# Hybrid decoder trunk on one core: maxima of weight strips over the partitions by a TensorE product and VectorE instead of GpSimd, and an earlier place for the maximum of a feed-forward strip

## The chip, the cores and the metric

The kernel runs on one core of one Trainium2 chip. The metric is the device time of one execution, in microseconds. A core has TensorE (PE, matrix products; its weight loads are shown apart as PEld), VectorE (DVE), ScalarE (ACT), GpSimdE (POOL) and the queues that issue transfers (SP's and POOL's among them). Each engine works through its own list of instructions in order and waits on semaphores of the others.

## The reference

Two layers of a decoder trunk in float32 over 1024 prompt tokens with 16 meta tokens ahead of them, and 8 running sequences of one token each. Each layer is a mixer and a feed-forward net, each with a norm before and after it:

```python
def sq_relu_mlp(x, w1, w2):
    h = jax.nn.relu(x @ w1)
    return (h * h) @ w2

h = rms_norm(x, p["norm_mix_pre"][i])
m = ssd_mixer(h, ...) if i % 2 == 0 else rglru_mixer(h, ...)   # layer 0 / layer 1
x = x + rms_norm(m, p["norm_mix_post"][i])
h = rms_norm(x, p["norm_ffn_pre"][i])
x = x + rms_norm(sq_relu_mlp(h, w1[i], w2[i]), p["norm_ffn_post"][i])
```

The width is 1024, the feed-forward width 4096. Prompt and sample tokens go through the kernel together, 1048 columns in three chunks of 350, 350 and 348.

## The kernel before

**Stages.** The core runs four stages one after the other: the SSD mixer, feed-forward net 0, the LRU mixer, feed-forward net 1. In the profile the SSD mixer takes about the first 930 us, feed-forward net 0 lies between 930 and 1700, the LRU mixer between 1700 and 2080, and the rest is feed-forward net 1.

**Products in float16 parts.** Every float32 operand is split in a float16 part hi and the rest lo, after a scaling by a power of two that makes it fit. A product takes three passes: hi by hi, hi by lo, lo by hi.

**Strips.** The weights come in strips of 256 columns, `[128, 8 x 256]` float32, 1 MB each, into the ring `ws` of two buffers. For each strip its largest magnitude is found (`rm`, the maxima on each partition; `wgb`, the maximum over the partitions on all of them). From it come the scale `sw` and its inverse `winv` by way of `qw` and `pw` (one column each, on DVE), and the strip is converted to the tile `wh` (hi by ACT, lo by DVE). The list `specs` gives the order of the strips and their kind: `a` takes a bound from the sums that ACT accumulates, `d` and `h` take the largest magnitude by one DVE reduce of 128 x 2048, `s` one that a kind `g` found long before.

**The feed-forward net.** It runs in four blocks of 1024 hidden units. A block has four strips of the first weight (kind `h` in block 0, `H` in the others) and then four of the second (kind `S` in blocks 0 to 2, `2` in block 3). Kinds `H` and `S` are multiplied by Winograd's form, seven products for eight. For these, three quarters of the strip are converted as they are into the tile `wp` (hi by ACT, lo by DVE), then POOL forms four sums in the room of the strip (`ws<-ws`), and the sums are converted into `wh`. All four pairs of K tiles of an `H` strip are summed, two of the four pairs of an `S` strip. Kinds `S` and `2` also carry the factors `rj` of the hidden rows, so their maximum is a reduce in two halves (`r4`), a product with `rj` and a small reduce (`rm`). One unit of an `H` or `S` strip is one chunk of tokens; a strip has three units. In a unit DVE adds the products up from PSUM into `z` (rows `z<-z,mm`), and then come the square of the hidden units (`H`, and `HT`, their sums) or the addition to the output `acc`. In block 0 POOL also forms the sums of the input (`f`), and where hidden units are summed, POOL's rows `z<-z` do it.

**Who sets the order.** The strips' pipeline is the generator `wlane`: it is advanced by one step (`tick`) beside each bundle of products, and `wneed` runs it on until the strip is there. It loads strip i+1 and then converts strip i. Within what dependences allow, a scheduler orders each engine's list anew, so the order on an engine isn't that of the program text. Almost every instruction is issued through one helper, so nearly all of them carry line L89 in the profile, and the names of the tiles tell them apart.

**The maximum over the partitions.** In `strip_scale` it is a library function of POOL, `partition_all_reduce`, of one column. There are 109 strips with such a maximum: 33 before feed-forward net 0, 32 in each feed-forward net, and 12 in the LRU mixer.

Of the kernel before, what the change touches and what calls it, by code (L numbers as in the profile page):

```python
# [11 lines left out]
F16 = mybir.dt.float16  # L12
I32 = mybir.dt.int32
AF = mybir.ActivationFunctionType
OP = mybir.AluOpType
AX = mybir.AxisListType
# [20 lines left out]
NSUM = 2  # L37
RBUF = 4
# [15 lines left out]
def cols(c):  # L54
    """The columns of a chunk of tokens."""
    return slice(c * CW, c * CW + WC[c])


class Carve:
    """Small float32 tiles cut from larger ones."""  # L60
# [17 lines left out]
class Queue:  # L78
    """An engine; while hold is set its instructions are issued in program order, and later ones behind them."""
# [38 lines left out]
class Body:  # L118
# [7 lines left out]
    # ------------------------------------------------------- order of work  # L126
    def tick(self):
        """One step of every piece of work that runs beside the matrix products."""
        for lane in list(self.lanes):
            if next(lane, self) is self:  # L130
                self.lanes.remove(lane)
# [5 lines left out]
    def tab(self, *args, **kw):  # L137
        """An activation whose function needs a table set: these stay in program order."""
# [13 lines left out]
    # ---------------------------------------------------------------- setup  # L152
    def setup(self):
# [28 lines left out]
        # pre-norm gains and group-norm gains scaled by a power of two so that hi/lo fit float16  # L182
# [13 lines left out]
        # the inputs of the ffn leave room for sums of four  # L196
# [48 lines left out]
    def pow2(self, b, n, pool, tag):  # L245
        """p = the power of two at or below b; s = 2^14 / p."""
# [9 lines left out]
    # -------------------------------------------------------------- weights  # L256
# [5 lines left out]
    def strip_scale(self, gmax):  # L262
        nc, ty = self.nc, self.tiny
        gb = ty.tile([P, 1], F32, tag="wgb", name="wgb")
        nc.gpsimd.partition_all_reduce(gb, gmax, P, RED.absmax)
        s, p = self.pow2(gb, 1, ty, "w")
        inv = ty.tile([P, 1], F32, tag="winv", name="winv", bufs=8)
        nc.vector.tensor_scalar(inv, p, 2.0 ** -14, None, op0=OP.mult)
        return s, inv, gb

    def split(self, w, st, s, parts):
        """w = float16 hi and lo parts of st * s, s [P, parts] by contiguous column ranges."""
# [12 lines left out]
    def wconv(self, st, kind, cols=SW):  # L285
        """A strip of weights as float16 hi and lo parts [P, 2, KT, cols], the factor that undoes its scaling and,
        for kinds h and H, the factor of its hidden units. Kind a takes a bound from the sums of the magnitudes, kind s
        one that kind g found before; kinds 2 and S carry the factors of the hidden rows. Kinds H and S are for the
        products by Winograd's form: with the quarters that are used as they are."""
        nc, ty = self.nc, self.tiny  # L290
        w = self.wh.tile([P, 2, KT * cols], F16, tag="wh", name="wh") if kind != "g" else None
        if kind in "HS":
            npair = 4 if kind == "H" else NSUM
            wp = self.wh.tile([P, 2, KT * cols], F16, tag="wh", name="wp")[:, :, :3 * npair * P]
            wp = wp.rearrange("p s (q k c) -> p s q k c", q=3, c=P)
        rm = ty.tile([P, 1], F32, tag="rm", name="rm")
        parts = 1
        if kind == "a":
            nc.scalar.activation(w[:, 0], st, AF.Abs, accum_out=rm)
# [25 lines left out]
        yield  # L325
        if kind in "HS":
            s, inv = self.quarter(s, inv)
# [12 lines left out]
    def quarter(self, s, inv):  # L340
        """Scales that leave room for sums of four."""
# [7 lines left out]
    def sums(self, wp, st, s, npair, parts):  # L349
        """Steps: the quarters of a strip [K tiles, M] that are used as they are, A11, A12, A22 (A ij: m tile i, k  # L350
        tiles of parity j), as float16 parts in wp; then the sums of Winograd's form in the room of the strip. Only
        the first npair pairs of k tiles."""
# [20 lines left out]
    def product(self, ps, i, w, B, T, npair):  # L373
        """ps = one of the seven products of quarters over the first pairs of k tiles, three passes of the float16
        parts; open for the products of the other pairs where there are any."""
# [14 lines left out]
    def quadrant(self, w, B, npair, i, l):  # L390
        """The operands of m tile i by half l of the tokens over the other pairs."""
# [7 lines left out]
    def wlane(self):  # L399
        def load(src, kind, cols=SW):  # L400
# [3 lines left out]
        for i in range(len(self.specs)):  # L404
            cost = {"H": 2, "S": 2, "g": 0}.get(self.specs[i][1], 1)
# [4 lines left out]
            yield from self.wconv(*staged.pop(i))  # L410
# [7 lines left out]
    def hidden_scale(self, wmax, inv):  # L418
        """The factors of one strip's hidden units: t = 2^7, or 2^6 where the squares are summed, / (power of two at or
        below the bound on the values before the square, the norm of the input times that of a column); returns  # L420
        t / (scales of the product); 1 / t^2 goes to rj."""
# [6 lines left out]
        nc.vector.tensor_scalar(lb, wmax, self.gbound[:, gi:gi + 1], 32.0, op0=OP.mult, op1=OP.mult)  # L428
# [14 lines left out]
    def summed(self, b, s):  # L443
        """Whether the hidden units of a strip of block b enter the second product by Winograd's form."""
# [7 lines left out]
    def bundle(self, ps, w, m, act, c, kts=range(KT), first=True, last=True):  # L452
        """ps += sum over k of w[k, m tile]^T act[k, chunk c], three passes of the float16 parts."""
# [1205 lines left out]
```

## Time and profile before

| what | value |
|---|---|
| median of 3 runs | 2842.84 us (2841.06 to 2843.44) |
| profiled execution, first to last instruction (span) | 2836.7 us |
| mean granted TensorE clock in it | 0.968 |
| busy: PE, DVE, ACT, POOL | 2583.1, 2110.1, 1322.6, 691.4 us |
| all-reduces of strips on POOL (`wgb<-rm` in the profile's groups) | 100 of 555 ns |
| loads of feed-forward and mixer-output strips (`ws<-w`) | 64 of 1024 KB, 4.9 us from issue to landing (median) |

The profiled execution gives its span, which excludes what lies around the first and the last instruction; the median of the runs lies 6.1 us above that span. Busy time of an engine is a share of the whole span; the stages have different limits, so the prediction reads it by stage.

### The profile page before, as it was taken

The page shows a single profiled execution, that of the slowest core. Times are in us where ns is not written, and L with a number is a line of the kernel's source. Part 1 is how long each engine was busy: PE and PEld are TensorE (multiplying, and loading weights), DVE is VectorE, ACT ScalarE, POOL GpSimd, SP SyncE. Part 2 cuts the span into 40 slices and gives each one's busy share as a digit, 9 for nine tenths or more (in the row PEclk, how much of TensorE's full clock was granted, in tenths as well). Part 3 has the DMA queues.
Part 4 walks back from the last instruction along what each step waited for, and adds up shares of the span by engine and source line. Part 5 has one row for each costly group of instructions (what it writes and reads, how often), then busy time and mean ns, then how long its engine had stood idle before and what let it go on. Part 6 is the DMA issues. An engine that isn't in the chain of part 4 may idle for free. (4 is left out here: it accounts for less than half of the span.)

```text
span 2836.7 us, 56933 instructions
## 1 busy us (share of the span) xinstructions
PE 2583.1 (91%) x23209; PEld 2060.6 (73%) x23209; DVE 2110.1 (74%) x5043; ACT 1322.6 (47%) x2148; POOL 691.4 (24%) x972
## 2 busy tenths in 40 slices
PE   4999999999999999789989999979999779989998
PEld 2666666666666667789989976646667779989976
DVE  4889778977873685568778788787685667878776
ACT  4655455545544354344253344658564335253352
POOL 2222111212212024442232201123014452231301
PEclk9999999999999999889999999989999989999999
DMA  3232233223345320101122123110220101111122
GB/s 123 99 119 90 87 107 115 102 88 108 113 159 187 117 106 31 46 31 46 61 72 79 46 110 113 63 62 33 89 108 31 46 31 46 47 45 53 54 73 95
DMA packets 52758, 229.15 MB, mean 81 GB/s; under 512 B 9056, under 2 KB 18416, under 8 KB 31632
## 3 DMA queue, kind: packets, MB, share of 16 engines
q1 hardware_dynamic: 46112, 190.81, 19.1%
q0 software_dynamic: 6384, 34.71, 3.1%
q8 instruction: 181, 2.97, 0.4%
q14 instruction: 81, 0.66, 0.1%
HBM read 186.28 MB, written 39.22 MB: 79 GB/s over the span
## 5 line engine op out<-in xcount | busy, mean ns | idle before, releaser
L89 PEld LDWEIGHTS <-wh 128*128 128x128 f16 x17040 | 1504.0, 99 | 503.7 <-issue 54.7
L89 PE MATMUL mm<-U,wh 128*128 128x350 f16 (+3 forms) x7056 | 989.4, 297 | 20.7 <-ACT rr L89 13.2
L89 PE MATMUL mm<-H,wh 128*128 128x175 f16 (+5 forms) x5664 | 557.7, 253 | 35.3 <-DVE z L89 30.4
L89 PEld LDWEIGHTS <-wp 128*128 128x128 f16 x3888 | 311.0, 99 | 87.6 <-issue 60.5
L89 POOL TENSOR_TENSOR ws<-ws 128x256 f32<-128x256 f32 (+1 forms) x192 | 205.2, 1069 | 328.6 <-DVE wp L89 214.4
L89 DVE TENSOR_TENSOR z<-z,mm 128x175 f32<-128x175 f32 (+3 forms) x648 | 228.4, 370 | 29.2 <-ACT z L89 22.0
L89 POOL PARTITION_ALL_REDUCE wgb<-rm x100 | 55.5, 555 | 656.6 <-issue 338.4
L89 PE MATMUL mm<-U,wp 128*128 128x175 f16 (+1 forms) x1728 | 154.8, 245 | 55.2 <-DVE z L89 55.1
L89 PE MATMUL mm<-TT,wh 128*128 128x175 f16 (+1 forms) x1728 | 167.0, 248 | 10.2 <-ACT TT L89 9.3
L89 ACT ACTIVATE z<-z,ti 128x700 f32<-128x700 f32 (+1 forms) x72 | 63.0, 875 | 183.5 <-DVE z L89 183.5
L89 DVE SCALAR_TENSOR_TENSOR wh<-ws,sw,wh 128x1024 f16<-128x1024 f32 x94 | 122.0, 1320 | 28.3 <-ACT wh L89 28.3
L89 DVE TENSOR_SCALAR qw<-wgb 128x1 f32<-128x1 f32 x103 | 15.5, 150 | 167.3 <-POOL wgb L89 167.1
L89 DVE SCALAR_TENSOR_TENSOR wh<-ws,s,wh 128x256 f16<-128x256 f32 x256 | 114.7, 490 | 11.1 <-ACT wh L89 11.1
L89 DVE TENSOR_REDUCE rm<-ws 128x1 f32<-128x2048 f32 x40 | 91.3, 2281 | 31.2 <-DMA ws<-w 26.7
L89 PE MATMUL mm<-H,wp 128*128 128x175 f16 (+1 forms) x864 | 90.5, 241 | 25.5 <-DVE z L89 23.1
L89 DVE TENSOR_TENSOR ss<-ss,sqt 128x350 f32<-128x350 f32 (+3 forms) x154 | 75.9, 500 | 41.8 <-ACT sqt L89 41.1
L89 ACT ACTIVATE wh<-ws,s 128x512 f16<-128x512 f32 x128 | 83.0, 710 | 48.0 <-POOL ws L89 23.2
L89 DVE SCALAR_TENSOR_TENSOR conv<-pre,ssmall,conv 128x1072 f32<-128x1072 f32 x78 | 103.8, 1330 | 0.1
L89 ACT ACTIVATE wh<-ws,sw 128x2048 f16<-128x2048 f32 x47 | 93.7, 1993 | 14.5 <-DVE sw L89 11.7
L89 DVE TENSOR_SCALAR L<-L,ncs 128x128 f32<-128x128 f32 (+1 forms) x288 | 90.6, 357 | 13.2 <-DMA L<-csd 13.2
L89 DVE TENSOR_TENSOR H<-z,H 128x175 f16<-128x175 f32 (+5 forms) x120 | 81.2, 694 | 23.6 <-ACT H L89 19.5
L89 ACT ACTIVATE pre<-mm,undo 128x8 f32<-128x8 f32 (+1 forms) x104 | 46.5, 474 | 110.7 <-PE mm L89 110.7
(279 smaller groups left out, 4176.9 us busy)
## 6 DMA issues: line engine op xcount, KB each, us to landing
ws<-w SPq DMA_DIRECT2D x64, 1024.0 KB, 4.9
ws<-w_ssd_in SPq DMA_DIRECT2D x24, 1024.0 KB, 5.4
L<-csd SPq DMA_DIRECT2D x64, 256.0 KB, 3.2
ws<-w_lru_in SPq DMA_DIRECT2D x12, 1024.0 KB, 4.9
xd<-xc POOLq DMA_DIRECT2D x6, 1400.0 KB, 5.5
xc<-xd SPq DMA_DIRECT2D x6, 1400.0 KB, 6.0
h<-ssd_h SPq DMA_DIRECT2D x8, 1024.0 KB, 4.9
bc<-bcd SPq DMA_DIRECT2D x8, 1024.0 KB, 4.8
```

Of the source, the lines that this page charges most:

```text
L89: r = f(*args, **kw)
```

## The change

`strip_scale` no longer calls POOL. TensorE multiplies the upper halves of `rm` (its float32 numbers read as bfloat16, the column repeated over 128 columns) by the identity, which puts the 128 maxima side by side on every partition of a PSUM tile, and DVE reduces the 128 columns into `wgb`. The maximum is then cut to bfloat16, which leaves its power of two as it was; the constant 32.0 in the bound on the hidden units becomes 32.3 for that. For the kinds `h`, `H`, `S` and `2`, `wlane` now runs the strip's maximum and scale before it waits for room and before it loads the next strip; the tiles `wh` and `wp` are taken only after the scale. Two other all-reduces (of the norm gains, and of the gates of the LRU mixer) stay on POOL. The rest of the difference takes out comments.

```diff
     def strip_scale(self, gmax):
         nc, ty = self.nc, self.tiny
+        ps = self.mm()
+        nc.tensor.matmul(ps[:, :P], gmax.bitcast(BF16)[:, 1:2].to_broadcast([P, P]), self.ident.bitcast(BF16)[:, 1::2], start=True, stop=True)
         gb = ty.tile([P, 1], F32, tag="wgb", name="wgb")
-        nc.gpsimd.partition_all_reduce(gb, gmax, P, RED.absmax)
+        nc.vector.tensor_reduce(gb, ps[:, :P], axis=AX.X, op=OP.max)
...
     def wconv(self, st, kind, cols=SW):
-        w = self.wh.tile([P, 2, KT * cols], F16, tag="wh", name="wh") if kind != "g" else None
-        if kind in "HS":
-            npair = 4 if kind == "H" else NSUM
-            wp = self.wh.tile([P, 2, KT * cols], F16, tag="wh", name="wp")[:, :, :3 * npair * P]
-            wp = wp.rearrange("p s (q k c) -> p s q k c", q=3, c=P)
+        new = lambda name: self.wh.tile([P, 2, KT * cols], F16, tag="wh", name=name)
...
         if kind == "a":
+            w = new("wh")
             nc.scalar.activation(w[:, 0], st, AF.Abs, accum_out=rm)
...
         s, inv, gb = self.strip_scale(rm)
-        yield
+        yield EARLY
+        if kind != "a":
+            w = new("wh")
         if kind in "HS":
+            npair = 4 if kind == "H" else NSUM
+            wp = new("wp")[:, :, :3 * npair * P].rearrange("p s (q k c) -> p s q k c", q=3, c=P)
             s, inv = self.quarter(s, inv)
...
     def wlane(self):
         for i in range(len(self.specs)):
+            conv = None
+            if self.specs[i][1] in "hH2S":
+                conv = self.wconv(*staged.pop(i))
+                while next(conv) is not EARLY:
+                    yield
             cost = {"H": 2, "S": 2, "g": 0}.get(self.specs[i][1], 1)
             while self.ready and sum(len(r[0]) if isinstance(r[0], tuple) else 1 for r in self.ready) + cost > self.ahead:
                 yield
             if i + 1 < len(self.specs):
                 staged[i + 1] = load(*self.specs[i + 1])
-            yield from self.wconv(*staged.pop(i))
+            yield from conv or self.wconv(*staged.pop(i))
             yield
...
     def hidden_scale(self, wmax, inv):
-        nc.vector.tensor_scalar(lb, wmax, self.gbound[:, gi:gi + 1], 32.0, op0=OP.mult, op1=OP.mult)
+        nc.vector.tensor_scalar(lb, wmax, self.gbound[:, gi:gi + 1], 32.3, op0=OP.mult, op1=OP.mult)
```

The numbers behind the names below tell buffers apart (they differ between the two kernels); a row is the line in the source, the operation, output and inputs, the shape, and how many stand together.

**DVE, the last `S` strips of block 1 in feed-forward net 0, before.** `ws_14669`, `ws_15033` and `ws_15397` are three strips that follow each other; `qw_15839` is the first step of the scale of `ws_15397`.

```order
L89 SCALAR_TENSOR_TENSOR wh_15035<-ws_14669,s4_15231,wh_15035 128x256
L89 SCALAR_TENSOR_TENSOR wp_15400<-ws_15033,s4_15595,wp_15400 128x128 x3
L89 TENSOR_TENSOR z_15004<-z_15004,mm_15002 128x2x175
L89 SCALAR_TENSOR_TENSOR wp_15400<-ws_15033,s4_15595,wp_15400 128x128 x3
L89 TENSOR_TENSOR z_15004<-z_15004,mm_15003 128x175 x2
L89 SCALAR_TENSOR_TENSOR acc_10692<-z_15004,iq4_14865,acc_10692 128x700
L89 TENSOR_TENSOR z_15118<-z_15118,mm_15114 128x175
L89 TENSOR_REDUCE rm_15765<-ws_15397 128x1
L89 TENSOR_TENSOR z_15118<-mm_15115,z_15118 128x2x175
L89 TENSOR_TENSOR z_15118<-z_15118,mm_15115 128x175
L89 TENSOR_TENSOR z_15118<-z_15118,mm_15116 128x2x175
L89 TENSOR_SCALAR qw_15839<-wgb_15837 128x1
```

Straight behind the last lo part of one strip stand the lo quarters of the next (its scale was found earlier), then the maximum of the third and its scale.

**DVE at the same place in the program, after.** `ws_14883` and `ws_15249` and `ws_15615` are three strips that follow each other; `wgb_15239` (ahead of these rows) and `wgb_15605` are the maxima of the first and the second.

```order
L91 TENSOR_SCALAR pw_15243<-qw_15241 128x1
L91 TENSOR_SCALAR sw_15245<-pw_15243 128x1
L91 TENSOR_SCALAR winv_15247<-pw_15243 128x1
L91 TENSOR_SCALAR sq4_15253<-sw_15245 128x1
L91 TENSOR_SCALAR iq4_15255<-winv_15247 128x1
L91 TENSOR_SCALAR s4_15257<-rj_13267,sq4_15253 128x4
L91 SCALAR_TENSOR_TENSOR wp_15252<-ws_14883,s4_15257,wp_15252 128x128 x3
L91 TENSOR_TENSOR z_15208<-z_15208,mm_15206 128x2x175
L91 SCALAR_TENSOR_TENSOR wp_15252<-ws_14883,s4_15257,wp_15252 128x128 x3
L91 SCALAR_TENSOR_TENSOR wh_15251<-ws_14883,s4_15257,wh_15251 128x256 x4
```

From the scale to the quarters `wp` to the sums' lo parts `wh` of the same strip there is now one row `z` of other work. The same engine a little later, from the first strip's last lo parts to the second strip's scale:

```order
L91 TENSOR_TENSOR z_15345<-z_15345,mm_15344 128x174 x2
L91 SCALAR_TENSOR_TENSOR acc_10776<-z_15345,iq4_14889,acc_10776 128x2x348
L91 TENSOR_TENSOR z_15464<-z_15464,mm_15460 128x175
L91 TENSOR_REDUCE rm_15859<-ws_15615 128x1
L91 TENSOR_TENSOR z_15464<-mm_15461,z_15464 128x2x175
L91 TENSOR_TENSOR z_15464<-z_15464,mm_15461 128x175
L91 TENSOR_TENSOR z_15464<-z_15464,mm_15462 128x2x175
L91 TENSOR_TENSOR z_15464<-z_15464,mm_15463 128x175 x2
L91 SCALAR_TENSOR_TENSOR acc_10776<-z_15464,iq4_15255,acc_10776 128x700
L91 TENSOR_TENSOR z_15574<-z_15574,mm_15570 128x175
L91 TENSOR_TENSOR z_15574<-mm_15571,z_15574 128x2x175
L91 TENSOR_REDUCE wgb_15605<-mm_15603 128x1
```

The maximum of the third strip (`rm_15859`), whose buffer the first strip leaves, now stands ahead of the scale of the second (`wgb_15605`); the quarters of the second follow only behind that.

**POOL in the same blocks, before.** Rows `ISA` without a tile load a library of POOL functions, the row `ISA wgb<-rm` is the all-reduce.

```order
L89 TENSOR_TENSOR ws_14669<-ws_14669 128x2x128 x4
L89 ISA
L89 ISA wgb_15511<-rm_15401 128x1
L89 ISA
L89 TENSOR_TENSOR ws_15033<-ws_15033 128x2x128 x4
L89 ISA
L89 ISA wgb_15837<-rm_15765 128x1
L89 ISA
L89 TENSOR_TENSOR ws_15397<-ws_15397 128x4x128 x4
```

Around each all-reduce the library is loaded and the one for ordinary rows loaded again. After, the same stretch holds only:

```order
L91 TENSOR_TENSOR ws_14141<-ws_14141 128x2x128 x4
L91 TENSOR_TENSOR ws_14549<-ws_14549 128x2x128 x4
L91 TENSOR_TENSOR ws_14883<-ws_14883 128x2x128 x4
L91 TENSOR_TENSOR ws_15249<-ws_15249 128x2x128 x4
L91 TENSOR_TENSOR ws_15615<-ws_15615 128x4x128 x4
L91 TENSOR_TENSOR z_16190<-z_16190 128x175 x4
```

**PE, after.** `rm_15127` holds the maxima of `ws_14883`; the strip's own first product comes 156 matmuls further on.

```order
L91 MATMUL mm_15205<-HT_10777,wh_14885 128x175
L91 LDWEIGHTS rm_15127
L91 MATMUL mm_15237<-ident_83,rm_15127 128x128
L91 LDWEIGHTS wh_14885
L91 MATMUL mm_15206<-H_13260,wh_14885 128x175
L91 LDWEIGHTS wh_14885
```

The added product stands in the stream of the strip ahead, between two products of a unit. Over the whole program PE gets 109 weight loads and 109 matmuls more, DVE 109 reduces more, POOL has 160 `ISA` rows and 109 all-reduces fewer (1141 rows before, 872 after), and SP and ACT have as many as before in another order.

More of the change, by code (lines that the diff above doesn't have):

```diff
@@ L12 @@
 F16 = mybir.dt.float16
+BF16 = mybir.dt.bfloat16
 I32 = mybir.dt.int32
@@ L37 @@
 NSUM = 2
+EARLY = "scale found"
 RBUF = 4
```

## The prediction

> **What bounds the kernel now.** I began with the page's busy times and costliest groups:
>
> ```profile
> PE 2583.1 (91%) x23209; PEld 2060.6 (73%) x23209; DVE 2110.1 (74%) x5043; ACT 1322.6 (47%) x2148; POOL 691.4 (24%) x972
> ...
> L89 POOL PARTITION_ALL_REDUCE wgb<-rm x100 | 55.5, 555 | 656.6 <-issue 338.4
> ...
> L89 DVE TENSOR_SCALAR qw<-wgb 128x1 f32<-128x1 f32 x103 | 15.5, 150 | 167.3 <-POOL wgb L89 167.1
> ...
> ws<-w SPq DMA_DIRECT2D x64, 1024.0 KB, 4.9
> ```
>
> PE is the busiest engine, at 91%, but not everywhere. POOL stands idle 656.6 us ahead of its all-reduces, 338.4 of them in issue, and DVE then idles 167.1 us ahead of `qw`, the first step after the maximum. I took the stretch of feed-forward net 0 where strips are converted, 24 strips, cut where PE first uses a group's first strip: `S` of block 0, `H` and `S` of block 1, `H` and `S` of block 2, `H` of block 3 (length, busy time and instructions of PE, PEld, DVE, ACT, POOL, then the clock):
>
> ```profile
> 1094.60:1211.90 117.30, 94.19 (x1082) 91.71 (x1081) 70.56 (x178) 41.84 (x81) 59.50 (x86) 0.88 0.10 37
> 1211.90:1312.10 100.20, 84.77 (x1011) 82.98 (x1010) 70.80 (x177) 49.46 (x84) 35.81 (x51) 0.91 0.12 43
> 1312.10:1397.20 85.10, 82.82 (x1081) 81.97 (x1081) 68.46 (x178) 24.90 (x50) 18.08 (x20) 1.00 0.15 51
> 1397.20:1494.30 97.10, 82.64 (x1012) 80.52 (x1010) 74.13 (x179) 46.97 (x78) 29.85 (x41) 0.95 0.19 67
> 1494.30:1581.50 87.20, 83.97 (x1081) 81.83 (x1082) 72.56 (x181) 24.75 (x50) 21.67 (x24) 1.00 0.20 73
> 1581.50:1668.40 86.90, 79.78 (x1010) 78.12 (x1007) 69.22 (x169) 42.73 (x63) 14.30 (x14) 0.98 0.19 70
> ```
>
> The `S` groups of blocks 1 and 2 are bound by PE: 82.8 of 85.1 us busy, clock 1.00, 21.5 us a strip. The others aren't. `S` of block 0 takes 29.3 us a strip, `H` 25.0, 24.3 and 21.7. All six take 573.8 us for 6277 matmuls. The best 50 us, against one of the worst, show what PE can do:
>
> ```profile
> 1200.00:1250.00 50.00, 42.52 (x479) 41.35 (x478) 32.31 (x81) 19.98 (x30) 21.19 (x27) 0.84 0.06 22
> 1300.00:1350.00 50.00, 48.80 (x636) 47.98 (x634) 41.66 (x116) 21.72 (x47) 7.92 (x12) 1.00 0.16 58
> ```
>
> At 636 matmuls in 50 us the 6277 need 493 us. So 80 us in this net, and as many in the other, could be won at most; that is the whole room for a gain there.
>
> The strips' pipeline explains both kinds of group. POOL and then DVE (start, duration, and in brackets the idle time before), at the last `S` strips of block 1:
>
> ```profile
> 1327.53 3.15 POOL L89 TENSOR_TENSOR ws<-ws 128x256 f32<-128x256 f32 x4 [10.50 <-DVE wp L89]
> 1336.77 0.41 POOL L89 PARTITION_ALL_REDUCE wgb<-rm  x1 [6.09 <-issue]
> 1348.66 3.68 POOL L89 TENSOR_TENSOR ws<-ws 128x256 f32<-128x256 f32 x4 [11.49 <-DVE wp L89]
> ```
>
> ```profile
> 1333.51 0.15 DVE L89 TENSOR_REDUCE rm<-r4s 128x1 f32<-128x4 f32 x1
> ...
> 1337.21 0.15 DVE L89 TENSOR_SCALAR qw<-wgb 128x1 f32<-128x1 f32 x1 [2.98 <-POOL wgb L89]
> ...
> 1341.05 1.67 DVE L89 SCALAR_TENSOR_TENSOR wh<-ws,s,wh 128x256 f16<-128x256 f32 x4
> ...
> 1343.52 0.94 DVE L89 SCALAR_TENSOR_TENSOR acc<-z,iq,acc 128x696 f32<-128x696 f32 x1
> 1344.38 0.33 DVE L89 TENSOR_TENSOR z<-z,mm 128x175 f32<-128x175 f32 x1
> 1344.62 0.48 DVE L89 SCALAR_TENSOR_TENSOR wh<-ws,s,wh 128x256 f16<-128x256 f32 x1
> 1345.02 0.52 DVE L89 TENSOR_TENSOR z<-mm,z 128x350 f32<-128x350 f32 x1
> ...
> 1346.09 0.48 DVE L89 SCALAR_TENSOR_TENSOR wh<-ws,s,wh 128x256 f16<-128x256 f32 x1
> 1346.49 0.87 DVE L89 SCALAR_TENSOR_TENSOR wp<-ws,s,wp 128x128 f16<-128x128 f32 x3
> ...
> 1351.60 2.29 DVE L89 TENSOR_REDUCE rm<-ws 128x1 f32<-128x2048 f32 x1 [1.21 <-DMA ws<-w]
> ```
>
> Around its all-reduce of 0.41 us POOL loses 6.09 us ahead, in issue (the library), and the DVE rows it serves can't begin. Yet this stretch runs at full PE rate. The reason is the order on DVE: the lo quarters of the next strip (1346.49) follow the last `wh` directly, so that POOL's sums (1348.66) and ACT's hi parts run while the load (1346.57 to 1351.60, 5.0 us), the maximum and the all-reduce of the strip behind it run. The loop from one last `wh` to the next is then: load 5.0, maximum 2.4, all-reduce and `qw` 3.6 (1333.66 to 1337.21), scale and rows `z` 3.8 (to 1341.05), `wh` with rows between 5.5 (to 1346.57): 20.3 us, just under PE's 21.
>
> Where POOL has `z` or `f` rows as well, the reloads delay them. An instance, PE in block 1:
>
> ```profile
> 1258.05 1.90 PE L89 MATMUL mm<-U,wp 128*128 128x174 f16 x12 [5.81 <-DVE z L89]
> ```
>
> It waits 5.81 us for a DVE `z`, in a window at clock 0.84.
>
> **The change, part by part.** *Removed:* 109 all-reduces with their reloads. Each costs POOL about 12 us: 6.09 ahead, and as much behind it before an ordinary row can run (an estimate: the way back is like the way there). Nothing is put in their place on POOL. The Trainium skill's "GPSIMD Engine Reference", section 2.1, gives about 6 us (5.95) for a first call to freshly loaded code; the 6.09 above agrees. Its section 4.1 assigns a reduction along the partitions to GpSimd, a rule against this change; the trace bears it out for the 0.41 us alone, not with the reload.
>
> *Added:* a product and a reduce per strip. Nearest rows, a product of 128x128 float32 and a DVE operation on 128x128 of PSUM:
>
> ```profile
> L89 PE MATMUL cb<-conv 128*128 128x128 f32 x128 | 25.4, 280 | 0.0
> ...
> L89 DVE TENSOR_TENSOR cbm<-cb,tri 128x128 f32<-128x128 f32 x64 | 17.8, 277 | 0.0
> ```
>
> So 0.28 us on DVE. For PE the ends are 0.08 us (50 us over 636) and 0.28; I take 0.2 with its weight load. For 48 strips in the stretches below it is in the chain; for the other 61 it makes 61 x 0.2 = 12 us on PE at most. Against that stand waits which go, in the SSD mixer:
>
> ```profile
> DVE qw L89 <- POOL wgb L89: 15.7, 5, 11.7
> ```
>
> I set these two against each other, 0 in sum, ends -16 and +20 (12 us, and half of 33 reduces of 0.28 where DVE is full).
>
> *Moved:* the order, and here lies the sum. In the new order (the two DVE places shown with the change) the scale of a strip stands behind the last `wh` of the strip ahead, and even behind the maximum of the strip after it, which needs the buffer just freed. Only then come the quarters, the sums on POOL, ACT's hi parts and `wh`, with one `z` row in between. What ran beside load and maximum now comes after them. Rows for its links (behind the bar the busy time in us and the mean of one in ns):
>
> ```profile
> L89 POOL TENSOR_TENSOR ws<-ws 128x512 f32<-128x512 f32 x96 | 129.9, 1353 | 160.9 <-DVE wp L89 87.4 <-issue 68.8
> ...
> L89 DVE TENSOR_REDUCE rm<-ws 128x1 f32<-128x2048 f32 x40 | 91.3, 2281 | 31.2 <-DMA ws<-w 26.7 <-DMA ws<-w_lru_out 2.5 <-DMA ws<-w_lru_in 1.8
> ...
> L89 POOL TENSOR_TENSOR ws<-ws 128x256 f32<-128x256 f32 x96 | 75.3, 785 | 167.7 <-DVE wp L89 127.0 <-issue 27.4 <-DVE z L89 8.1
> ...
> L89 DVE SCALAR_TENSOR_TENSOR wp<-ws,sq,wp 128x512 f16<-128x512 f32 x72 | 53.6, 758 | 0.0
> ...
> L89 ACT ACTIVATE wp<-ws,sq 128x512 f16<-128x512 f32 x72 | 47.9, 712 | 88.2 <-DVE sh L89 40.7 <-PE mm L89 32.4 <-issue 9.0
> L89 ACT ACTIVATE wh<-ws,sq 128x2048 f16<-128x2048 f32 x24 | 47.9, 1994 | 51.9 <-POOL ws L89 51.9
> ...
> L89 ACT ACTIVATE wp<-ws,s 128x128 f16<-128x128 f32 x144 | 47.0, 389 | 47.6 <-DVE s L89 28.2 <-issue 19.4
> ```
>
> An `S` strip after, from last `wh` to last `wh`: load 5.0; maximum 2.4 (in two halves; in one, 2.28); the rows `z` and `acc` up to `wgb` 3.1 (in the DVE rows above, starts step by 0.24 for a `z` of 175, 0.43 for 350, 0.86 for `acc`); `wgb` 0.3; five steps of scale 0.9 (0.15 to 0.2 each); six hi quarters on ACT 6 x 0.389, 2.3, DVE's lo quarters beside them; sums on POOL 4 x 0.785, 3.1; first hi part on ACT 0.7 (as for 512 columns in the row of the `H` quarters); `wh` with the rows between 5.5. Sum 23.3 against 21.5, the mean of the two groups: 8 strips x 1.8 = +14 us.
>
> An `H` strip: load 5.0; maximum 2.3; `HT` and `z` 0.9; `wgb` and a `z` 0.5; steps to the scale 0.6; three lo quarters 2.0 (0.67 from start to start), with five more steps, `H` and `z` between them 2.6; sums on POOL 4 x 1.353, 5.4; hi of the whole strip 2.0; two `wh` of 1.3 with `H` and `z` between 3.8. Sum 25.1. Blocks 1 and 2: 8 x 25.1 = 201 against 197.3, +4. Block 3 has no `HT`, 24.1: 96 against 86.9, +9.
>
> `S` of block 0: the chain is 23.3, but POOL also forms input sums there (59.5 us busy in the group's 117.3). Ends 23.3 and 29.3; I take 25.5, since the reloads go but the sums still queue behind `f`: 102 against 117.3, -15. The four strips `2`: the added product now comes 34 to 48 matmuls ahead of the strip's first use on PE, about 3 us, so some of the conversion is bare; ends 0 and 2 us a strip, I take 0.8, +3.
>
> Sum per net 14 + 4 + 9 - 15 + 3 = +15, for two nets +30 (the second net runs the same program on strips of the same size). The profiled span 2836.7 becomes 2867; the median stands 6.1 us above it, so 2873.
>
> What I cost at nothing: SP's loads keep their number and still wait for a buffer to be freed, with the other loads of SP behind them as before; taking `wh` and `wp` later only frees room; 32.3 and the cut to bfloat16 change no work. PE's matmuls behind the added one wait if `rm` is late. Then z rows come late too; in the chains above the product is done while DVE does the rows up to `wgb`, so this hides behind 2 to 3 us of DVE, and costs up to 2 us a strip if PE arrives first.
>
> **The rivals.** *A, faster: the loop is shorter than PE's time.* If POOL's sums and ACT's parts overlap more than the order suggests (the links are summed end to end, and each overlap of 2 us counts 48 times), all stretches fall to PE's 493 us plus 24 x 0.2: -75 per net, 2693. For it: DVE idles long in the slow groups, 70.6 of 117.3 us busy. Against: the load and the maximum are in the loop for certain. It decides where an `S` strip's loop gets under 21.3 and an `H` strip's under 20.
>
> *B, faster in part:* the reloads' stretches recover, the rest holds. `S` of block 0 at 23.3 (-24), `H` of blocks 1 and 2 at 23.2 (midway to the 21.7 of block 3, where POOL has no `z`; -12), the others as before: -36 per net, 2771. For it: the clock under 1 in just these groups. Against: the 25.1 above.
>
> *C, slower still: PE's pauses bring the clock down.* If every strip leaves PE idle for 3 to 5 us, the clock goes as in the window at 0.84 with 479 matmuls. A strip of 21.1 us becomes 25.1 and 2 us of pause stay: 27 x 24 = 648 against 573.8, +74 per net, 2991. For it: only the windows with long stalls show a clock under 1. The Trainium skill's "TensorE: Matmul & The Clock Gate", Part 1, has the clock fall after an idle window of about 3.4 us; the 5.81 us stall in the 0.84 window agrees. Against: the waits come mostly as pieces of 1 to 3 us between units.
>
> *D, nothing:* loss and gain cancel, 2843.
>
> **How the numbers follow.** The forecast 0.50, A 0.17, B 0.17, C 0.08, D 0.08. The forecast's own range is 2835 to 2940 (1 us on each of the 48 strips is 48 us, and the ends above); C lies beyond. Leaving out C and the lower part of A, 2725 to 2940 holds about 0.8. Faster is A and B, 0.34; within 0.2% (5.7 us, about what a measurement of this kernel can tell from no change) D, 0.08; slower the forecast and C, 0.58.
>
> **What would show it.** Right: gaps of POOL before all-reduces and `qw` behind POOL gone; in `S` of blocks 1 and 2 some 23 us a strip, DVE idle about 4 us ahead of `wh` with ACT as releaser, and some 3 us ahead of `rm` with the load as releaser; `S` of block 0 under 27. Wrong: PE at 636 matmuls per 50 us in those groups (A), or clock 0.9 and less in most of them (C). I would be wrong above all if DVE's order leaves less serial than the rows tell, since 48 strips multiply each link.

## The result and the profile after

The changed kernel takes 2916.6 us (median of 4 runs, 2906.1 to 2920.7) against 2843.1 for the kernel before: 1.0258 times, interval 1.0233 to 1.0283. The forecast of 2873 had the direction, but less than half the loss: 30 us forecast, 73.5 measured. The measured time lies inside the stated range of 2725 to 2940.

From the page of the profile after, the busy times and the groups that changed:

```profile
PE 2636.0 (90%) x23318; PEld 2089.8 (72%) x23318; DVE 2184.9 (75%) x5152; ACT 1329.8 (46%) x2148; POOL 668.5 (23%) x863
...
L91 POOL TENSOR_TENSOR ws<-ws 128x256 f32<-128x256 f32 (+1 forms) x192 | 214.1, 1115 | 656.5 <-DVE wp L91 602.9
...
L91 PE MATMUL mm<-TT,wh 128*128 128x175 f16 (+1 forms) x1728 | 191.0, 262 | 119.1 <-ACT wh L91 80.7
L91 DVE SCALAR_TENSOR_TENSOR wh<-ws,s,wh 128x256 f16<-128x256 f32 x256 | 141.5, 596 | 29.9 <-ACT wh L91 29.7
```

POOL now waits for DVE's quarters (602.9 us in the view of the waits) and no longer for its library. What stands against that are idle times which before were small: PE ahead of the products of `TT` with `wh` waits 119.1 us, most of it for ACT's `wh`. In the kernel before the same group has:

```profile
L89 PE MATMUL mm<-TT,wh 128*128 128x175 f16 (+1 forms) x1728 | 167.0, 248 | 10.2 <-ACT TT L89 9.3
```

There PE's longest wait is another, 113.2 us in all for DVE's `z`. The same six groups of feed-forward net 0 as in the prediction, from first use to first use:

```profile
1097.60:1195.00 97.40, 88.95 (x1087) 86.13 (x1085) 71.93 (x179) 38.44 (x80) 55.84 (x78) 0.93 0.10 34
1195.00:1302.60 107.60, 85.52 (x1016) 82.80 (x1014) 77.99 (x181) 51.47 (x82) 37.47 (x45) 0.89 0.12 40
1302.60:1393.40 90.80, 85.67 (x1086) 83.47 (x1085) 72.63 (x183) 22.56 (x50) 15.34 (x17) 0.98 0.14 48
1393.40:1503.70 110.30, 88.09 (x1015) 85.14 (x1013) 79.57 (x178) 50.31 (x78) 31.54 (x37) 0.88 0.17 59
1503.70:1608.40 104.70, 92.81 (x1088) 90.18 (x1086) 79.25 (x192) 23.71 (x52) 18.95 (x20) 0.90 0.18 61
1608.40:1709.60 101.20, 84.57 (x1016) 81.48 (x1015) 67.36 (x158) 44.17 (x62) 16.96 (x13) 0.92 0.13 44
```

| group (us) | before, net 0 | after, net 0 | forecast difference | difference, net 0 | difference, net 1 |
|---|---|---|---|---|---|
| `S` of block 0 | 117.3 | 97.4 | -15 | -19.9 | -16.7 |
| `H` of blocks 1 and 2 | 197.3 | 217.9 | +4 | +20.7 | +20.7 |
| `S` of blocks 1 and 2 | 172.3 | 195.4 | +14 | +23.1 | +11.3 |
| `H` of block 3 | 87.0 | 101.2 | +9 | +14.2 | +17.4 |
| strips `2` (in net 1 to the end) | 88.4 | 93.5 | +3 | +5.1 | +4.1 |
| sum | | | +15 | +43.2 | +36.8 |

The two nets give 80 us instead of 30, and 47 of the missing 50 are in the `H` groups. The other stages, from first use to first use, give -3, and the time to the first product of a strip is 5 us longer: together the 82.1 us by which the spans of the two profiled executions differ.

What the added instructions take (busy us, mean ns):

```profile
L91 DVE TENSOR_REDUCE wgb<-mm 128x1 f32<-128x128 f32 x103 | 29.3, 285 | 24.9 <-PE mm L91 24.7
...
L91 PE MATMUL mm<-ident,rm 128*128 128x128 bf16 x99 | 21.8, 221 | 12.7 <-DVE rm L91 12.4 <-ACT wh L91 0.2
```

The product takes 0.22 us on PE and the reduce 0.285 on DVE, against 0.2 and 0.28 in the sum.

### The profile page after: what moved, and what is told of

It reads as the page before. It is cut to its first block, busy times and chain, and to the rows that moved or that the text cites. A ratio compares the mean times of both kernels' runs of the same rounds, so it can differ in the third digit from the quotient of the medians.

```text
span 2918.8 us, 56796 instructions
## 1 busy us (share of the span) xinstructions
PE 2636.0 (90%) x23318; PEld 2089.8 (72%) x23318; DVE 2184.9 (75%) x5152; ACT 1329.8 (46%) x2148; POOL 668.5 (23%) x863
## 5 line engine op out<-in xcount | busy, mean ns | idle before, releaser
L91 PEld LDWEIGHTS <-wh 128*128 128x128 f16 x17040 | 1534.1, 100 | 639.5 <-ACT wh L91 104.5
L91 PE MATMUL mm<-U,wh 128*128 128x350 f16 (+3 forms) x7056 | 1015.2, 301 | 12.2 <-ACT rr L91 11.6
L91 PE MATMUL mm<-H,wh 128*128 128x175 f16 (+5 forms) x5664 | 569.4, 255 | 8.9 <-DVE wh L91 8.8
L91 POOL TENSOR_TENSOR ws<-ws 128x256 f32<-128x256 f32 (+1 forms) x192 | 214.1, 1115 | 656.5 <-DVE wp L91 602.9
L91 PE MATMUL mm<-TT,wh 128*128 128x175 f16 (+1 forms) x1728 | 191.0, 262 | 119.1 <-ACT wh L91 80.7
L91 DVE SCALAR_TENSOR_TENSOR wh<-ws,s,wh 128x256 f16<-128x256 f32 x256 | 141.5, 596 | 29.9 <-ACT wh L91 29.7
L91 PE MATMUL mm<-HT,wh 128*128 128x175 f16 (+1 forms) x864 | 102.8, 248 | 39.4 <-DVE wh L91 22.8
L91 ACT ACTIVATE z<-mm 128x175 f32<-128x175 f32 x144 | 43.7, 303 | 173.9 <-PE mm L91 173.9
L91 DVE TENSOR_TENSOR H<-z,H 128x175 f16<-128x175 f32 (+5 forms) x120 | 90.8, 773 | 33.8 <-ACT z L91 18.1
L91 DVE SCALAR_TENSOR_TENSOR wh<-ws,sq,wh 128x1024 f16<-128x1024 f32 x48 | 61.5, 1282 | 63.4 <-ACT wh L91 63.4
L91 DVE TENSOR_SCALAR L<-L,ncs 128x128 f32<-128x128 f32 (+1 forms) x288 | 93.5, 369 | 8.3 <-DMA L<-csd 8.3
L91 DVE TENSOR_TENSOR ss<-ss,sqt 128x350 f32<-128x350 f32 (+3 forms) x154 | 76.5, 504 | 29.5 <-ACT sqt L91 28.7
```

Source lines behind the costliest of these rows:

```text
L91: r = f(*args, **kw)
```

## The experiments

Theory at the start: the loss is a serial chain, and it is there because the product of a strip's scale is an instruction of PE's stream, whose place the program text sets, while POOL's all-reduce could be moved ahead freely. Rivals: the new order of scale, room and load makes the loss; the load and DVE's order make it, as the prediction had it; PE's pauses and the clock make it. Times are medians, and each ratio is to runs of the kernel before on the same chip.

**The old generator, with product and reduce.**

```diff
-            if self.specs[i][1] in "hH2S":
-                conv = self.wconv(*staged.pop(i))
-                while next(conv) is not EARLY:
-                    yield
...
-            yield from conv or self.wconv(*staged.pop(i))
+            yield from self.wconv(*staged.pop(i))
```

> The changed kernel with the old generator: a strip's maximum and scale come after the wait for room and after the load of the next strip, and wh and wp are taken first, as in the kernel before; only the engines of the maximum over the partitions are the new ones. Theory (the place of the product in PE's stream makes the loss): the product stands at the same place on PE, 156 to 180 matmuls ahead of the first use for H and S strips, so about the time of the changed kernel, 2895 to 2925 us. Rival (the new order of scale, room and load makes the loss): 2840 us or less, since the reloads on POOL are gone.

Measured 2920.9 us, 1.0294 times (1.0271 to 1.0318), group by group within 3 us of the changed kernel. (The edit changes `wlane` alone: unlike what the expectation says, `wh` and `wp` are still taken after the scale, as in the changed kernel.) So the second half of the change, the earlier maximum, does nearly nothing; the loss comes with the first half.

**POOL's all-reduce, with the new generator.**

```diff
-        ps = self.mm()
-        nc.tensor.matmul(ps[:, :P], gmax.bitcast(BF16)[:, 1:2].to_broadcast([P, P]), self.ident.bitcast(BF16)[:, 1::2], start=True, stop=True)
         gb = ty.tile([P, 1], F32, tag="wgb", name="wgb")
-        nc.vector.tensor_reduce(gb, ps[:, :P], axis=AX.X, op=OP.max)
+        nc.gpsimd.partition_all_reduce(gb, gmax, P, RED.absmax)
```

> The changed kernel with POOL's all-reduce instead of product and reduce; the new order of scale, room and load stays. Theory (place on PE): the all-reduce is not tied to a place in PE's stream, so the time falls back near the kernel before, 2825 to 2860 us. Rival (new order): 2900 us or more, with the reloads on top.

Measured 2832.8 us, 0.9982 times (0.9965 to 0.9999): the kernel before. With the run ahead this settles that the change of engines, not of the generator, loses the time in the order that the kernel came with.

**The next strip's scale between sums and `wh`.**

```diff
...
+            for step in conv:
+                if step == SUMS and early(i + 1):
+                    yield from find(i + 1)
+                yield
```

> The changed kernel, but the maximum and scale of the next strip (kinds h, H, S, 2) are put between the sums of a strip and the parts wh made of them, so that PE's product stands a whole strip earlier (252 to 270 matmuls ahead of the first use, not 156 to 180). Theory (place on PE): H strips fall from 26.7-28 us to 20-21 and S strips of block 1 from 22.9 to 21.3; only S of block 2 in net 0 keeps its 26, since gate strips stand between; 2760 to 2800 us in all. Rival (the loop goes through the load and DVE, as the prediction had it): the load still follows the last wh, so over 2880 us.

Measured 2881.7 us, 1.0158 times (1.0136 to 1.018): some 30 us of the loss gone, not more. The place in PE's stream seems to be a part, as the product now stands a whole strip further ahead (in the traces too), but the rival was right that the chain stays. DVE of this kernel at `S` strips of block 1:

```profile
1309.15 0.48 DVE L92 SCALAR_TENSOR_TENSOR wh<-ws,s,wh 128x256 f16<-128x256 f32 x1
...
1314.64 1.22 DVE L92 TENSOR_REDUCE r<-ws 128x2 f32<-128x1024 f32 x1 [2.86 <-DMA ws<-w]
...
1318.88 0.28 DVE L92 TENSOR_REDUCE wgb<-mm 128x1 f32<-128x128 f32 x1
...
1322.12 1.52 DVE L92 SCALAR_TENSOR_TENSOR wp<-ws,s,wp 128x128 f16<-128x128 f32 x5 [0.47 <-ACT wp L92]
...
1331.68 0.48 DVE L92 SCALAR_TENSOR_TENSOR wh<-ws,s,wh 128x256 f16<-128x256 f32 x1
```

Between the last `wh` of a strip (to 1309.6) and the next quarters (1322.12) stand the load (5.0 us), the maximum that waits for it and the scale behind that.

**POOL's sums left out.** The products then use unsummed quarters, so the output is another one.

```diff
...
-            tt(o, a, b, op=op)
...
```

> The changed kernel without POOL's four sums of a strip (the products then use unsummed quarters; all else stays). They take 5.8 us of an H strip and 3.1 us of an S strip. Theory (serial chain from scale to wh): all of it comes off, H strips 28 to 22-23 us, S strips 22.9 to 21.3 (PE's own time), about 2775 to 2800 us. Rival (PE's pauses and the clock, not the chain, make the time): at most a third of it, over 2860 us.

Measured 2726.8 us, 0.961 times (0.9584 to 0.9635): 190 us less than the changed kernel, and below the theory's 2775 to 2800. `H` of block 1 falls from 107.6 to 88.0, of block 3 from 101.2 to 77.0; `S` of block 1 falls to 86.0, where PE is nearly the limit. That is 4.9 to 6.1 us an `H` strip, for sums that take 5.8, as much as if they stood fully in the chain. Rows of DVE which run beside the sums get shorter without them as well; this run doesn't tell the two apart.

**The gate strips earlier.** They have only a load and a maximum, and stand between the `S` strips of block 2 in net 0. Here one stands ahead of each `h` strip of block 0.

```diff
-                sp += [(a["w1"][l, 4 * b + s], "H" if b else "h") for s in range(4)]
                 for s in range(4):
-                    if (l, b) == (0, 2):
+                    if (l, b) == (0, 0):
                         sp.append((a["w_lru_in"][4 + s], "g"))
+                    sp.append((a["w1"][l, 4 * b + s], "H" if b else "h"))
+                for s in range(4):
                     sp.append((a["w2"][l, 4 * b + s], "S" if b < 3 else "2"))
```

> The changed kernel with the four gate strips (load and maximum only) moved from between the S strips of block 2 in net 0 to ahead of the strips h of block 0. Theory (the gates' loads and maxima stand in the serial chain there): S of block 2 in net 0 falls from 104.7 us to the 90.9 of net 1, and nothing else changes: 2900 to 2906 us. Rival (net 0 is slower there for another reason): no change, 2917 us.

Measured 2904.4 us, 1.0252 times (1.0231 to 1.0272). `S` of block 2 in net 0 falls from 104.6 to 90.6 us, as the theory says. But something else changes too: `H` of block 3 behind it rises from 101.2 to 107.3, so the six groups of net 0 win 8 us and not 14. Why was not followed. The whole time is 12.2 us less than that of the changed kernel, but it ran on another chip and the two ratios' intervals overlap, so it is the group that tells. In the kernel before the same gates cost 2 us there (87.2 against 85.2 in net 1).

**Product and reduce twice.**

```diff
         gb = ty.tile([P, 1], F32, tag="wgb", name="wgb")
+        nc.vector.tensor_reduce(gb, ps[:, :P], axis=AX.X, op=OP.max)
+        ps = self.mm()
+        nc.tensor.matmul(ps[:, :P], gb.bitcast(BF16)[:, 1:2].to_broadcast([P, P]), self.ident.bitcast(BF16)[:, 1::2], start=True, stop=True)
+        gb = ty.tile([P, 1], F32, tag="wgb2", name="wgb2")
         nc.vector.tensor_reduce(gb, ps[:, :P], axis=AX.X, op=OP.max)
```

> The changed kernel with a second product and a second reduce behind the first of each strip (of the number already found, so the value stays). Theory (the chain is serial, so each link counts in full): 0.22 us for the product, 0.28 for the reduce and some 0.2 of waits for each of 24 strips a net: 25 to 40 us more, 2942 to 2957 us. Rival (the added instructions hide): under 8 us more.

Measured 2928.2 us, 1.0336 times (1.0314 to 1.0358): 11.6 us more by the times, 22 by the ratios (0.78%), between the two theories. PE waits 76.5 us for the first reduce ahead of the second product, but its waits for `wh` fall in turn, from 167 to 115 us. So the chain isn't without slack, and the added instructions by themselves aren't the loss of 73.5.

**Scale ahead, the maximum before the quarters.** Here and in the next, `find` runs a strip's maximum and scale without a step between, and the gates stand among the `h` strips as above.

```diff
...
+            yield
+            if self.specs[i][1] in "HS2":
+                find(i + 1)
+            yield from convs.pop(i) if i in convs else self.wconv(*staged.pop(i))
```

> As the one before it, but the maximum and scale of the next strip are issued ahead of the quarters of this one, so that on DVE the maximum, with its wait for the load, stands between a strip's last wh and the next strip's quarters. The product stands 420 to 450 matmuls ahead of the first use. Theory of two places (PE's product, and the maximum ahead of the quarters on DVE): the load of 5.0 us and the maximum stay in the chain, S strips about 22 us, H strips 23 to 25, 2790 to 2870 us. Rival (only the place on PE matters): the same time as with the quarters first, 2700 to 2760 us.

("The one before it" is the next experiment here.) Measured 2821.2 us, 0.9949 times (0.9935 to 0.9963). The product stands far ahead on PE now, and with the gates away the six groups of net 0 fall from 612.0 to 568.4 us. Yet `H` of block 1 still takes 102.2 us and `S` of block 1 89.9.

**Scale ahead, the quarters and sums before the maximum.**

```diff
...
+            if self.specs[i][1] in "HS":
+                while next(conv) is not SUMS:
+                    pass
+            if self.specs[i][1] in "HS2":
+                find(i + 1)
+            yield
+            yield from conv
```

> Product and reduce stay, the order is another: when there is room, the next strip is loaded, the quarters and POOL's sums of this strip are issued, then the maximum and scale of the next strip, then wh of this one; the four gate strips go ahead of the strips h of block 0. On DVE the quarters then follow the last wh of the strip ahead, ahead of the next maximum, as in the kernel before, and the product stands 456 to 516 matmuls ahead of the first use. Theory (the loss is the serial order on DVE and PE, not the product or the reduce): S strips 21.3 us, H strips 20 to 22, 2700 to 2760 us, below the kernel before. Rival (the product in PE's stream costs by itself, since PE waits at it for the maximum): S and H stay above the kernel before, 2845 us or more.

Measured 2714.2 us, 0.958 times (0.9564 to 0.9596): 107 us less than the kernel ahead, and 120 us less than the kernel before the change. Against the kernel ahead the order of two steps in the text is another, and the quarters and sums are now issued without a step of the generator between them; the two were not tried apart. The six groups:

```profile
1074.70:1164.00 89.30, 84.46 (x1085) 84.05 (x1084) 65.48 (x174) 36.24 (x72) 55.01 (x76) 0.96 0.11 37
1164.00:1256.40 92.40, 80.48 (x1016) 78.62 (x1014) 73.09 (x182) 50.26 (x84) 35.02 (x47) 0.98 0.13 47
1256.40:1340.80 84.40, 82.41 (x1087) 82.27 (x1085) 72.15 (x190) 27.07 (x51) 18.30 (x16) 1.00 0.14 52
1340.80:1427.00 86.20, 79.57 (x1015) 78.55 (x1013) 69.12 (x173) 45.35 (x78) 30.69 (x40) 0.98 0.15 51
1427.00:1511.40 84.40, 82.41 (x1086) 82.27 (x1085) 72.48 (x190) 27.04 (x51) 18.31 (x16) 1.00 0.15 51
1511.40:1593.20 81.80, 77.25 (x1018) 77.06 (x1016) 67.27 (x159) 41.12 (x62) 10.69 (x8) 1.00 0.23 83
```

518.5 us for what took 573.8 before and 612.0 after; `S` strips of blocks 1 and 2 at 21.1 us, clock 0.96 to 1.00. This version beats both kernels.

**The same order with POOL's all-reduce.**

```diff
-        ps = self.mm()
-        nc.tensor.matmul(ps[:, :P], gmax.bitcast(BF16)[:, 1:2].to_broadcast([P, P]), self.ident.bitcast(BF16)[:, 1::2], start=True, stop=True)
         gb = ty.tile([P, 1], F32, tag="wgb", name="wgb")
-        nc.vector.tensor_reduce(gb, ps[:, :P], axis=AX.X, op=OP.max)
+        nc.gpsimd.partition_all_reduce(gb, gmax, P, RED.absmax)
```

> The order with the quarters and sums first (which took 2714 us with product and reduce), but with POOL's all-reduce for the maximum. Theory (once the order no longer ties the scale to the chain, the reloads on POOL are what the change of engines saves): each strip again loses some 12 us of POOL, S of block 0 back to 29 us a strip and H of blocks 1 and 2 to 24-25, 2790 to 2830 us. Rival (the order alone makes the gain, the engine doesn't matter): 2710 to 2740 us.

Measured 2861.3 us, 1.0077 times (1.0058 to 1.0095). The theory is right on the direction and short on the size: the engines are worth 147 us in this order (141 by the ratios), 59 of them in the SSD mixer. The fastest version with the all-reduce is the one with the new generator (2832.8 us), and 2714.2 is 119 us less than that (114 by the ratios). The six groups of net 0 are back at 570.8, and POOL waits for its library as before:

```profile
L92 POOL PARTITION_ALL_REDUCE wgb<-rm x100 | 50.1, 501 | 690.9 <-issue 322.8
```

The mixer, from the first use of its first strip to that of the first `h` strip, takes 1016.4 us instead of 957.5, which leads to the next two runs. (By first uses the mixer ends at 1004 us in the kernel before and the LRU mixer begins at 1757, later than the bounds of the stages given with that kernel.)

**One more step between load and conversion, in the kernel before.**

```diff
+            yield
             yield from self.wconv(*staged.pop(i))
```

> The kernel before with one more step of the generator between the load of the next strip and the conversion of this one, as the order with the sums first has it (its SSD mixer took 957.5 us of span against 982.7). Theory: that step alone gives the mixer's 20 to 25 us: 2815 to 2822 us. Rival (the mixer gains because its all-reduces left POOL): 2835 us or more.

Measured 2874.7 us, 1.0134 times (1.0119 to 1.0149). The theory fell: the mixer gets 30 us longer (1013.0 against 982.7). The time lies where the rival has it, but the rival didn't say that the step costs anything.

**The same step in the changed kernel,** for strips outside the nets:

```diff
+            if conv is None:
+                yield
             yield from conv or self.wconv(*staged.pop(i))
```

> The changed kernel with one more step of the generator between the load of the next strip and the conversion of this one, for the strips outside the feed-forward nets alone. The same step made the SSD mixer of the kernel before 30 us longer. Theory (with the maximum off POOL the step lets ACT and DVE start a conversion later, without a reload behind it, and this is where the sums-first order gets its shorter mixer): the mixer's span falls from 981.8 to 957-962 us, 2892 to 2898 us in all. Rival (the gate strips' new place or the rest of that order shortens the mixer): 975 us or more, 2910 to 2920 us.

Measured 2888.7 us, 1.0199 times (1.014 to 1.0258), the mixer 958.2. So the step costs 30 us with the all-reduce and gains 24 us with the product. Why it gains was not taken apart further.

**Product and reduce twice, sums first.** The second pair is added to the order with the sums first, as above.

> The order with the sums first (2714 us) and a second product and reduce behind the first of each strip. Theory (the scale now has slack, so the added instructions cost no more than their time on PE): 109 products of 0.1 to 0.2 us, 0 to 20 us more, 2714 to 2735 us. Rival (still a serial chain): 24 strips a net at 0.5 us or more, with waits 35 us more, 2749 us.

Measured 2771.8 us, 0.9771 times (0.9751 to 0.9791): some 55 us more, so the theory that slack hides them fell. The products that read `rm` and `wgb` (busy us, mean ns, then idle time before and who ended it), first with one product a strip and then with two:

```profile
L92 PE MATMUL mm<-ident,rm 128*128 128x128 bf16 x99 | 22.1, 224 | 51.2 <-DVE z L92 29.4 <-DVE rm L92 20.2 <-ACT wh L92 1.4
```

```profile
L92 PE MATMUL mm<-ident,wgb 128*128 128x128 bf16 x103 | 24.3, 236 | 107.4 <-DVE wgb L92 107.1
...
L92 PE MATMUL mm<-ident,rm 128*128 128x128 bf16 x99 | 21.9, 221 | 4.2 <-DVE rm L92 3.1 <-ACT wh L92 0.8 <-DVE sh L92 0.2
```

Of two products the first waits 4.2 us in all, the second 107.4, for the reduce. That is 60 us more idle time on PE than ahead of the single product, about what the kernel takes longer, against 24.3 us for the added products themselves. So most of it isn't the number of instructions: a product that needs a result which DVE has only just been asked for holds up what stands behind it on PE.

## Why the prediction was right and wrong

**The mechanism was right in the main:** a serial loop through the load, DVE's order and POOL's sums. What the prediction left open is which half of the change makes the order on DVE that it read; the first two runs show that it is the exchange of engines. The removed reloads gave back what was forecast where POOL was loaded: `S` of block 0, -15 forecast, -19.9 and -16.7 measured. The serial loop of an `S` strip was summed as 23.3 us; measured are 22.7 in block 1 (90.8 and 90.7 for four). Its links in the trace after, DVE and then POOL:

```profile
1327.43 1.67 DVE L91 SCALAR_TENSOR_TENSOR wh<-ws,s,wh 128x256 f16<-128x256 f32 x4
...
1334.04 2.35 DVE L91 TENSOR_REDUCE r<-ws 128x2 f32<-128x1024 f32 x2 [1.60 <-DMA ws<-w]
...
1339.34 0.28 DVE L91 TENSOR_REDUCE wgb<-mm 128x1 f32<-128x128 f32 x1
...
1343.31 3.09 DVE L91 SCALAR_TENSOR_TENSOR wh<-ws,s,wh 128x256 f16<-128x256 f32 x4
...
1347.78 0.49 DVE L91 SCALAR_TENSOR_TENSOR wh<-ws,s,wh 128x256 f16<-128x256 f32 x1 [0.88 <-ACT wh L91]
```

```profile
1343.47 3.52 POOL L91 TENSOR_TENSOR ws<-ws 128x256 f32<-128x256 f32 x4 [18.74 <-DVE wp L91]
```

From last `wh` (1329.1) the load takes until 1334.04, `wgb` comes at 1339.34, `wh` begins at 1343.31. The link that the sum had in the wrong place is the wait for POOL: four `wh` (the unsummed half) go first, beside the sums. So DVE idles 0.88 us ahead of `wh` with ACT as releaser where some 4 were named as a sign, and 1.60 for the load where 3 were.

**The step that failed is "An `H` strip: ... Sum 25.1".** Measured in net 0 are 26.9 in the mean of block 1, 27.6 in block 2, and 25.3 in block 3, where 24.1 was forecast. The term was too small; that it grows at all was right. One of the longer strips, of block 1, in the trace after, from last `wh` to last `wh` (1229.05 to 1258.15, 29.1 us); DVE, POOL, PE:

```profile
1227.77 1.28 DVE L91 SCALAR_TENSOR_TENSOR wh<-ws,sq,wh 128x1024 f16<-128x1024 f32 x1
...
1232.40 0.52 DVE L91 TENSOR_TENSOR z<-mm,z 128x350 f32<-128x350 f32 x1 [1.62 <-PE mm L91]
...
1235.66 0.35 DVE L91 TENSOR_TENSOR H<-z,H 128x174 f16<-128x174 f32 x1 [0.84 <-ACT H L91]
1235.94 2.27 DVE L91 TENSOR_REDUCE rm<-ws 128x1 f32<-128x2048 f32 x1
...
1238.99 0.28 DVE L91 TENSOR_REDUCE wgb<-mm 128x1 f32<-128x128 f32 x1
...
1239.99 0.15 DVE L91 TENSOR_SCALAR sq<-sw 128x1 f32<-128x1 f32 x1
...
1241.45 0.75 DVE L91 SCALAR_TENSOR_TENSOR wp<-ws,sq,wp 128x512 f16<-128x512 f32 x1
...
1244.97 0.42 DVE L91 TENSOR_TENSOR H<-z,H 128x175 f16<-128x175 f32 x1 [0.98 <-ACT H L91]
...
1245.56 0.76 DVE L91 SCALAR_TENSOR_TENSOR wp<-ws,sq,wp 128x512 f16<-128x512 f32 x1
1246.48 1.80 DVE L91 TENSOR_TENSOR HT<-z,HT 128x525 f16<-128x525 f32 x1 [0.17 <-ACT HT L91]
1248.20 0.32 DVE L91 TENSOR_TENSOR z<-z,mm 128x174 f32<-128x174 f32 x1
...
1254.56 0.34 DVE L91 TENSOR_TENSOR H<-z,H 128x175 f16<-128x175 f32 x1 [2.01 <-ACT H L91]
1254.82 1.28 DVE L91 SCALAR_TENSOR_TENSOR wh<-ws,sq,wh 128x1024 f16<-128x1024 f32 x1
1256.02 0.70 DVE L91 TENSOR_TENSOR HT<-z,HT 128x525 f16<-128x525 f32 x1
...
1256.88 1.27 DVE L91 SCALAR_TENSOR_TENSOR wh<-ws,sq,wh 128x1024 f16<-128x1024 f32 x1
```

```profile
1246.45 5.80 POOL L91 TENSOR_TENSOR ws<-ws 128x512 f32<-128x512 f32 x4 [0.68 <-ACT HT L91]
```

```profile
1224.38 0.48 PE L91 MATMUL mm<-TT,wh 128*128 128x175 f16 x2 [7.20 <-ACT wh L91]
...
1235.02 0.22 PE L91 MATMUL mm<-ident,rm 128*128 128x128 bf16 x1
...
1254.35 0.47 PE L91 MATMUL mm<-TT,wh 128*128 128x175 f16 x2 [5.43 <-ACT wh L91]
```

Against the sum, in this strip: load and wait until the maximum 6.9 us instead of 5.0. The maximum has no idle time for the load ahead of it; it stands behind rows `z` and `H` of the strip ahead, and before these DVE idles 3.9 us in all, for PE and ACT. From the maximum's start to the end of `sq` 4.2, 4.3 forecast with the rows between. The three quarters end 6.2 us after `sq`, not 4.6; ahead of the third stands an `H` that waits 0.98 us for ACT. The sums end 5.9 us behind that, not 5.4; then hi and `wh` as forecast. That makes 4.0 us in this strip; in the mean of the groups it is 1.8 us in block 1, 2.5 in block 2 and 1.2 in block 3. The strip ahead of this one (from 1198.3) takes 30.7 us: its load costs 5.0, as in the sum, but its quarters end 8.2 us after `sq`. Blocks 1 and 2 of both nets repeat this pair within 0.1 us in these links. So the part of the sum that was too small in both is the quarters with the rows `H`, `HT` and `z` between them: 8.2 and 6.2 us for 4.6, of which DVE stands idle 2.1 and 1.0, mostly for ACT. The sum counted such rows at their busy time.

Why those waits are there is argued, not shown: PE stands still 7.20 us at 1224.38 and 5.43 at 1254.35, for `wh`, so its products come late, the rows `z` and `H` behind them too, and with these the next strip. DVE's rows beside POOL's sums take longer as well (below), but in this strip DVE idles 2.01 us behind them (1254.56), so they don't lengthen the chain here. "PE's matmuls behind the added one wait if `rm` is late" looked at the wrong wait: PE idles 12.7 us ahead of the product itself in the whole span, while the strips' products wait for `wh`:

```profile
PE mm L91 <- ACT wh L91: 97.2, 36, 7.2
...
PE mm L91 <- DVE wh L91: 69.9, 82, 1.9
```

**A step was missing.** The sum for `S` of blocks 1 and 2 (+14) left out the four gate strips of net 0, whose loads and maxima stand in the chain: 23.1 in net 0, 11.3 in net 1, and moving them took the 104.6 us of the group to 90.6 (with the loss in the next group, told above).

**Rival C held in part.** The clock of the `H` groups fell to 0.89, 0.88 and 0.92 (0.91, 0.95, 0.98 before), and of `S` of block 2 to 0.90, not to the 0.84 that C was priced with. The `H` groups of blocks 1 and 2 have pauses of PE of 5 to 7 us. `S` of block 2 has none above 3.0 us, and yet the clock is 0.51 from 1532.7 to 1539.6, with a pause of 2.4 us there. The Trainium skill's "TensorE: Matmul & The Clock Gate", Part 1, has the clock fall after an idle window of about 3.4 us: the pauses in the `H` groups agree, the one of 2.4 us doesn't. Of the 34.9 us that the three `H` groups of net 0 take longer, the rows of the two tables give 11.0 as busy time of PE and 23.9 as time in which it isn't busy. A lower clock makes products longer, so as far as busy time tells, the pauses are the larger part. The prediction's row with the pause of 5.81 us (1252.24 to 1258.05) doesn't lie in its window at 0.84 but in the next 50 us, at 0.90; there the clock is 0.50 from 1256.8 to 1263.6.

**Rivals A, B and D** fell for the kernel as changed, but A's mechanism is there: once the order frees the scale, the gain of the removed reloads shows, and the two nets come to 518.5 and 520.5 us, against PE's 493.

What stays open: a third buffer for strips, which would take the load out of the chain, wasn't tried.

## What to carry to other kernels

A step that moves from an engine whose list the scheduler may rearrange to one whose order follows the text takes its place in that text with it (here PE: the product stands 156 to 180 matmuls ahead of most `H` and `S` strips in the trace after, 456 to 516 with the sums first, as was worked out from the text ahead of the runs): look at what then stands behind it, above all at the wait at its head, and write the step early in the text. Where a pipeline is a serial loop, write its links down from one event to the same event a period later, and count also the rows of other work that wait for the engine which the loop stops. Another order of two steps of a generator, with no step between the quarters and the sums, was worth 107 us here, more than the exchange of engines cost in the order that it came with.

## What the hardware showed beside this

DVE rows that read two SBUF operands slow down beside POOL's sums. Four `wh<-ws,s,wh` of 128x256 take 1.67 us at 1327.43 without POOL and 3.09 at 1343.31 with it; `HT<-z,HT` takes 1.80 at 1246.48 beside the sums, 0.70 at 1256.02 without. The `z<-z,mm` of 0.32 at 1248.20, which reads one operand from PSUM, is no longer beside the sums than elsewhere. The sums take longer too: 3.52 us for four at 1343.47, 3.15 in the kernel before at 1327.53. The Trainium skill's "GPSIMD Engine Reference", section 1, names SBUF interfaces shared with VectorE, with contention for instructions of two SBUF inputs; these rows agree and give the size. The mean of the group `wh<-ws,s,wh` rose from 490 ns to 596.
